# The first down projection of a decoder trunk: three column blocks token-major with seven block products in 17 chunks, results turned through DRAM

## The chip, the cores and the metric

The kernel runs on one core of one Trainium2 chip. It is one launch. The metric is the device time of that launch in microseconds, as the median of several runs. Before the change it is 2175.9 us (three runs, 2174.73 to 2176.43 us).

## The reference, cut to what matters

The reference computes a decoder trunk of two layers on 256 tokens of 2048 features, all in float32: a gated mixer layer, a convolutional feed-forward network (FFN), a shared key and value side, an attention layer, a second FFN, and a last RMS norm. The change is in the last step of the first FFN:

```
h = xn @ w_up                                    # [256, 11264]
h = conv(h);  gate, val = split(h)               # each [256, 5632]
return (silu(gate) * val) @ w_down               # [256, 5632] @ [5632, 2048], added to the residual
```

What follows it at once is the shared key side and the attention layer, which read the residual through two RMS norms with gains of their own (`kv_norm`, `b_norm`).

## The kernel before, in words

**Number format.** Every float32 operand of a matrix product is split into a rounded part and a remainder (`hi`, `lo`, type fp32r). A product of two operands is three matmuls: rounded by rounded, rounded by remainder, remainder by rounded. A weight matrix comes as chunks of 128 x 1024 floats (512 KB). ScalarE writes the rounded part of a chunk (L110), VectorE the remainder (L111), TensorE then has 24 matmuls of 256 columns for it.

**Two layouts.** In a *feature-major* block (`feat_block`) the weights are the stationary operand and the 256 tokens stream past; 256 output features come out as rows. In a *token-major* block (`tok_block`, `seven_block`) the activations are stationary and 512 weight columns stream past; tokens come out as rows. The residual `h` is kept feature-major, in 16 tiles of 128 features (`kt`), until the second FFN's end.

**What sets the order.** All weight chunks of the program are one list of items (`Stream`). The loop `run` goes through the list: at item *i* it loads item *i*+6, splits item *i*+3 and multiplies item *i*. Then it advances every pending generator by one `yield`: those are the evictions, norms and exchanges that follow a block. Each engine runs what it is given strictly in that order. An item made by `then` has no chunk: it calls a function (at its load or its multiply step), takes a place in the list, and advances no generator. There are four buffers for split chunks and four for loaded ones, three PSUM buffers for block results.

**Wide matmuls.** A call of `between` lets the next chunk run its first eight products, and the chunk after it two, as matmuls of 512 columns where others have 256 (two half-products in one instruction, or two of 256 columns in one).

**The first down projection.** `down0` is eight feature-major blocks of 11 chunks. At the end of block *p*, `residual` adds the result to two tiles of `h` (L394), multiplies them by the next gain and splits them into `X1` (`prep`, L309 on ScalarE, L310 on VectorE), and adds their squares to `acc` (L374, L379). After the last block, `token_scale` sums `acc` over features on TensorE (L407). The query projection `b_q`, token-major, reads `X1` right behind it.

**The second down projection** (`down1`) is done differently already: 1536 of its columns are three token-major blocks by `seven_block`, the rest `short_block` and `last_block`. In a block of 22 chunks, some chunks (`SUMMED`: one in the first block, eight in each of the others) are multiplied as a 2 x 2 block matrix product with seven products in place of eight (the scheme of Strassen and Winograd). Such a chunk is two items: nine matmuls on the chunk's own columns, twelve on sums of its columns; 21 in place of 24. VectorE makes the column sums (`weight_sums`, L492, L494, L495) and both items are split (L88, L89). The sums on the activation side are made once (`all_sums`, L471 to L481) and are kept in the room of `X1`. The results of `down1` stay token-major, since `h` has been turned by then.

**Turning.** `blocks_turned` transposes 32 x 32 blocks on VectorE (L853), `rows_out` writes the result to DRAM by four DMAs from SyncE's queue (L860), `rows_in` reads it back by one (L864). The mixer, the attention and `residual_by_token` use this way.

Of the kernel before, what the change touches and what calls it, by code (L numbers as in the profile page):

```python
# [10 lines left out]
F32 = mybir.dt.float32  # L11
F32R = mybir.dt.float32r
I32 = mybir.dt.int32
AF = mybir.ActivationFunctionType
# [162 lines left out]
def build(ctx, tc, d, out):  # L177
# [44 lines left out]
    def feat_block(src, x, K, done):  # L222

        box = {}
        n = K // 4
        for c in range(n):
            def mult(hi, lo, c=c):
                if c == 0:  # L230
                    box["ps"], box["both"] = main_ps(), False
                ps, xx, wide = box["ps"], x(), wide_next()
                box["both"] |= wide > 0

                def rounded(j, m):
                    nonlocal wide
                    w = hi[:, j * 256 + m * P:j * 256 + (m + 1) * P]
                    kt = 4 * c + j
                    if wide > 0:
                        mm(ps[:, m, :], w, xx[:, kt, :], kt == 0, False)  # L240
                        wide -= 1
                    else:
                        for half in range(2):
                            mm(ps[:, m, :T], w, xx[:, kt, half * T:(half + 1) * T], kt == 0 and half == 0, False)

                def remainder(j, m):
                    kt = 4 * c + j
                    mm(ps[:, m, :T], lo[:, j * 256 + m * P:j * 256 + (m + 1) * P], xx[:, kt, :T],
                       False, kt == K - 1)

                for product in (rounded, remainder):
                    for j in range(4):
                        for m in range(2):
                            product(j, m)
                if c == n - 1:
                    s.start(done(box["ps"], box["both"]))
            s.chunk(src[c], mult, FEAT_AT)
# [48 lines left out]
    def prep(dst, kt, gain):  # L306

        g = column(gain + kt)
        nc.scalar.activation(dst[:, kt, :T], h[:, kt, :], AF.Copy, scale=g)  # L309
        nc.vector.scalar_tensor_tensor(dst[:, kt, T:], h[:, kt, :], g, dst[:, kt, :T].bitcast(F32),  # L310
                                       op0=OP.mult, op1=OP.subtract)
# [78 lines left out]
    def residual(p, gain, scale=token_scale):  # L390

        def done(ps, both):
            hh = h[:, 2 * p:2 * p + 2, :]
            nc.vector.tensor_tensor(hh, hh, ps[:, :, :T], op=OP.add)  # L394
            if both:
                nc.vector.tensor_tensor(hh, hh, ps[:, :, T:], op=OP.add)
            for kt in (2 * p, 2 * p + 1):
                prep(X1, kt, gain)
            square_into_acc(p)
            yield  # L400
            if p == 7:
                yield from scale()
        return done
# [79 lines left out]
    def all_sums():  # L483
        for _ in range(4):
            yield
        for q in range(0, len(SUMMED), 2):
            yield from sums_of_blocks(q, SUMMED[q])
# [78 lines left out]
    def sums_into_residual(blk):  # L566
# [14 lines left out]
            state["summed"] += 1  # L581
        return done

    def short_block(src, x, K, done):

        n, box = K // 4, {}
        for c in range(n):
            def mult(hi, lo, c=c):
                if c == 0:
                    box["ps"] = main_ps()[:, :, :T]  # L590
                for tb in range(2):
                    short_products(box["ps"][:, tb, :], c, tb, x, K, hi, lo)
                if c == n - 1:
                    s.start(done(box["ps"]))
            s.chunk(src[c], mult, TOK_AT)
        return box
# [251 lines left out]
    def blocks_turned(src):  # L848


        n = src.shape[1]
        turned = ph.temp("turned", [P, 512])[:, :n * P].rearrange("p (c h j) -> p c h j", c=4, h=n)
        nc.vector.transpose(turned.rearrange("p c h j -> p h c j"), src.rearrange("p h (c i) -> p h c i", c=4))  # L853
        return turned.rearrange("p c h j -> p c (h j)")

    def rows_out(key, turned):

        way = dram.tile([4, 32, 4, turned.shape[2]], F32, name=f"way_{key}", tag=f"way_{key}")
        for r in range(4):
            nc.sync.dma_start(way[:, :, r, :].rearrange("c i x -> i c x"), turned[32 * r:32 * r + 32])  # L860
        return way

    def rows_in(dst, way):
        nc.sync.dma_start(dst, way.rearrange("c i r x -> (c i) r x"))  # L864
# [231 lines left out]
        return done  # L1096


    state = {"normed": False, "layer": 0, "v": 0, "done": 0, "gates": 0, "mixed": 0, "scaled": 0, "summed": 0, "wide": [8, 2]}
    cd = dram.tile([NH, T], F32, name="cd")  # L1100

    nc.scalar.dma_start(col[:, :C_KVNORM], d["col"][:, :C_KVNORM])
# [18 lines left out]
    for p in range(8):  # L1121
        feat_block(d["a_out"][4 * p:4 * p + 4], mlp_x2, KD, residual(p, C_FNORM, row_scale))
    ffn_up(0)
    for p in range(8):
        feat_block(d["down0"][11 * p:11 * p + 11], ffn_h, KF, residual(p, C_BNORM))

    s.then(at_mult=lambda: s.start(kv_operand()))
    for blk in range(4):
# [33 lines left out]
def tok_chunks(w):  # L1162

    K, N = w.shape
    a = w.reshape(K // 256, 2, P, N // 512, 512)
    return np.ascontiguousarray(a.transpose(3, 0, 2, 1, 4)).reshape(-1, P, CHUNK)
# [50 lines left out]
```

## Time and profile before

| | |
|---|---|
| median of 3 runs | 2175.9 us |
| the profiled execution's own time | 2175.67 us |
| its span, first to last instruction | 2173.8 us |
| TensorE matmul busy | 2164.6 us, 18689 instructions |
| VectorE busy | 1536.1 us (71%) |
| ScalarE busy | 1162.4 us (53%) |
| granted TensorE clock | 0.999 |
| DMA, mean | 206 GB/s |
| first down projection on TensorE | 753.54 to 992.90 us |
| second down projection on TensorE | 1932.24 to about 2166 us |

The busy time of an engine is read from the page's first part. A matmul's duration in the trace (276 ns for 256 columns) contains its way through the array; matmuls overlap, so their pace is read from the distance of their starts in the timeline. A line number such as L111 stands for the helper that records the operation, so one line can cover work of many stages.

### The profile page before, as it was taken

The page shows a single profiled execution, that of the slowest core. Times are in us where ns is not written, and L with a number is a line of the kernel's source. Part 1 is how long each engine was busy: PE and PEld are TensorE (multiplying, and loading weights), DVE is VectorE, ACT ScalarE, POOL GpSimd, SP SyncE. Part 2 cuts the span into 40 slices and gives each one's busy share as a digit, 9 for nine tenths or more (in the row PEclk, how much of TensorE's full clock was granted, in tenths as well). Part 3 has the DMA queues.
Part 4 walks back from the last instruction along what each step waited for, and adds up shares of the span by engine and source line. Part 5 has one row for each costly group of instructions (what it writes and reads, how often), then busy time and mean ns, then how long its engine had stood idle before and what let it go on. Part 6 is the DMA issues. An engine that isn't in the chain of part 4 may idle for free.

```text
span 2173.8 us, 45113 instructions
## 1 busy us (share of the span) xinstructions
PE 2164.6 (100%) x18689; PEld 2149.0 (99%) x18689; DVE 1536.1 (71%) x2188; ACT 1162.4 (53%) x1560; POOL 26.4 (1%) x46
## 2 busy tenths in 40 slices
PE   9999999999999999999999999999999999999998
PEld 9999999999999999999999999999999999999998
DVE  6696687777777745556787676678777777778884
ACT  6665555555555544444545665446555555555553
POOL 0000000000000000000001200000000000000000
PEclk9999999999999999999999999999999999999999
DMA  9686566666666666666777776667766666665674
GB/s 313 190 237 205 192 201 195 186 202 186 201 190 197 194 198 194 193 195 180 252 233 260 238 222 196 192 215 221 243 194 194 194 194 194 195 191 179 204 219 149
DMA packets 153230, 447.32 MB, mean 206 GB/s; under 512 B 25584, under 2 KB 44800, under 8 KB 152640
## 3 DMA queue, kind: packets, MB, share of 16 engines
q1 hardware_dynamic: 151488, 440.48, 64.6%
q0 software_dynamic: 1072, 3.41, 0.6%
q8 instruction: 146, 2.39, 0.5%
q10 hardware_dynamic: 464, 0.55, 0.1%
q14 instruction: 60, 0.49, 0.1%
HBM read 430.72 MB, written 13.65 MB: 204 GB/s over the span
## 4 chain that ended last, share of the span: by engine, by line
PE 100%; DVE 0%; ACT 0%; POOL 0%; issue 0%; DVEq 0%; POOLq 0%
PE ps L212 98%; PE mp L1074 0%; PE mp L682 0%; PE ps L1068 0%; PE ps L1069 0%; PE ps L1067 0%; PE mp L1073 0%; DVE h L649 0%; PE mp L407 0%; ACT sq L436 0%; PE mp L212 0%; DVE h L435 0%; DVE h L644 0%; ACT fin_t L636 0%; POOL ident L1109 0%
## 5 line engine op out<-in xcount | busy, mean ns | idle before, releaser
L111 DVE TENSOR_TENSOR wlo<-raw,whi 128x1024 fp32r<-128x1024 f32 x761 | 925.0, 1221 | 387.9 <-ACT whi L110 383.4
L110 ACT ACTIVATE whi<-raw 128x1024 fp32r<-128x1024 f32 x761 | 800.7, 1058 | 680.0 <-PE ps L212 592.8
L212 PE MATMUL ps<-X,whi 128*128 128x256 f32 (+1 forms) x6476 | 824.0, 279 | 0.0
L212 PEld LDWEIGHTS ps<-X,whi 128*128 128x128 f32 x6476 | 776.2, 188 | 6.5
L212 PE MATMUL ps<-X,wlo 128*128 128x256 f32 x3328 | 445.2, 276 | 0.0
L212 PEld LDWEIGHTS ps<-X,wlo 128*128 128x128 f32 x3328 | 409.8, 188 | 1.6
L212 PE MATMUL ps<-whi,ffn_H 128*128 128x256 f32 (+1 forms) x1232 | 200.9, 277 | 0.0
L212 PE MATMUL ps<-whi,X 128*128 128x256 f32 (+1 forms) x1136 | 183.3, 279 | 0.0
L212 PE MATMUL ps<-ffn_H,whi 128*128 128x256 f32 x1408 | 173.9, 276 | 0.0
L212 PEld LDWEIGHTS ps<-whi,ffn_H 128*128 128x128 f32 x1232 | 172.8, 188 | 0.4
L824 DVE SCALAR_TENSOR_TENSOR ffn_room<-ffn_room,col 128x255 f32<-128x255 f32 x352 | 161.8, 480 | 6.4
L212 PEld LDWEIGHTS ps<-ffn_H,whi 128*128 128x128 f32 x1408 | 166.1, 188 | 0.0
L212 PE MATMUL ps<-whi,att_X 128*128 128x256 f32 (+2 forms) x970 | 164.4, 285 | 0.0
L212 PEld LDWEIGHTS ps<-whi,X 128*128 128x128 f32 x1136 | 155.3, 188 | 1.4
L212 PE MATMUL ps<-wlo,ffn_H 128*128 128x256 f32 (+1 forms) x615 | 138.9, 277 | 0.0
L212 PEld LDWEIGHTS ps<-whi,att_X 128*128 128x128 f32 x970 | 135.3, 188 | 3.5
L388 DVE TENSOR_TENSOR ffn_room<-ps,rB 128x512 f32<-128x512 f32 x76 | 52.5, 691 | 116.2 <-PE ps L212 116.2
L820 ACT ACTIVATE ffn_room<-ffn_room,col 128x256 f32<-128x256 f32 x176 | 96.3, 595 | 50.0 <-DVE ffn_room L388 50.0
L212 PE MATMUL ps<-wlo,X 128*128 128x256 f32 (+1 forms) x566 | 116.7, 279 | 0.0
L212 PE MATMUL ps<-wlo,att_X 128*128 128x256 f32 (+2 forms) x476 | 105.5, 286 | 0.0
L212 PEld LDWEIGHTS ps<-wlo,ffn_H 128*128 128x128 f32 x615 | 101.1, 188 | 0.1
L212 PE MATMUL ps<-ffn_H,wlo 128*128 128x256 f32 x704 | 94.1, 276 | 0.0
(199 smaller groups left out, 1517.2 us busy)
## 6 DMA issues: line engine op xcount, KB each, us to landing
raw<-up SPq DMA_DIRECT2D x352, 512.0 KB, 4.1
raw<-down SPq DMA_DIRECT2D x154, 512.0 KB, 4.2
raw<-a_in_u SPq DMA_DIRECT2D x32, 512.0 KB, 4.3
raw<-a_out SPq DMA_DIRECT2D x32, 512.0 KB, 4.0
raw<-b_q SPq DMA_DIRECT2D x32, 512.0 KB, 4.8
raw<-kvf_v SPq DMA_DIRECT2D x32, 512.0 KB, 4.8
raw<-b_g SPq DMA_DIRECT2D x32, 512.0 KB, 4.6
raw<-b_out SPq DMA_DIRECT2D x32, 512.0 KB, 3.8
```

The lines of the kernel that those rows point to most:

```text
L110: self.nc.scalar.activation(h, raw, AF.Copy)
L111: self.nc.vector.tensor_tensor(l, raw, h.bitcast(F32), op=OP.subtract)
L212: nc.tensor.matmul(o, a, b, start=start, stop=stop, skip_group_check=True)
L388: nc.vector.tensor_tensor(a, src, rB[:, None, :].to_broadcast([P, 2, T]), op=OP.mult)
L820: nc.scalar.activation(c[:, m, :], a[:, m, :], AF.Identity, scale=w[2], bias=column(C_CONVB + l * 2 * KF + f))
L824: nc.vector.scalar_tensor_tensor(c[:, m, n:], a[:, m, :T - n], w[k], c[:, m, n:], op0=OP.mult, op1=OP.add)
```

## The change

The columns of `w_down[0]` are divided. The first 1536 are laid out token-major and are done by three calls of `seven_block`, as in the second down projection, with the same choice of chunks: 1 + 8 + 8 = 17 of 66 chunks are done with seven block products. The last 512 columns stay two feature-major blocks (*p* = 6 and 7) with `residual` as before.

The results of the three blocks come out token-major and the residual is feature-major, so they are turned: `sums_apart` first combines the block sums into a tile `Y` and adds the plain products (L593 to L604 of the changed kernel), `blocks_turned` and `rows_out` send each half of 128 tokens to DRAM, and `rows_added` reads it back and adds it to `h` (L621). That is six round trips. `residual_prepared` does for the twelve tiles of `h` what `residual` does at a block's end (`prep`, squares into `acc`), one step at a time, during the two feature-major blocks.

Five `then` items are new: `between` and the start of `all_sums` ahead of the three blocks, `between` and the start of `residual_prepared` behind them, and `check_prepared`, which asserts while the program is built that all twelve tiles are prepared, behind the last block.

```diff
@@ -580,6 +580,64 @@
             nc.vector.tensor_tensor(hh[:, :, T:], hh[:, :, T:], one[:, 0::2, :], op=OP.add)
             state["summed"] += 1
         return done
+
+    def sums_apart(blk):
+
+
+        box = {}
+
+        def sums(m):
+            Y = ph.temp("apart", [P, 4, T], bufs=1)
+            nc.scalar.activation(Y[:, 1, :], m[:, 0, :T], AF.Copy)
+            yield
+            nc.vector.tensor_tensor(Y[:, 0, :], Y[:, 1, :], m[:, 0, T:], op=OP.add)
+            nc.vector.tensor_tensor(Y[:, 3, :], Y[:, 0, :], m[:, 1, T:], op=OP.subtract)
+            yield
+            nc.vector.tensor_tensor(Y[:, 0::2, :], m[:, 1:, :T].to_broadcast([P, 2, T]), Y[:, 0::3, :], op=OP.subtract)
+            box["Y"] = Y
+
+        def done(ps):
+            while "Y" not in box:
+                yield
+            for tb in range(2):
+                z = box["Y"][:, 2 * tb:2 * tb + 2, :].rearrange("p a b -> p (a b)")
+                nc.vector.tensor_tensor(z, z, ps[:, tb, :], op=OP.add)
+                yield
+                turned = blocks_turned(z.rearrange("p (h x) -> p h x", h=4))
+                yield
+                s.start(rows_added(blk, tb, rows_out(f"d{blk}{tb}", turned)))
+                yield
+
+        return done, sums
+
+    def rows_added(blk, tb, way):
+        for _ in range(3):
+            yield
+        rows = ph.temp("drows", [P, 512]).rearrange("p (r x) -> p r x", r=4)
+        rows_in(rows, way)
+        for _ in range(5):
+            yield
+        hh = h[:, 4 * blk:4 * blk + 4, tb * P:(tb + 1) * P].rearrange("p h (r j) -> p r h j", r=4)
+        nc.vector.tensor_tensor(hh, hh, rows.rearrange("p r (h j) -> p r h j", h=4), op=OP.add)
+        state["added"] += 1
+
+    def residual_prepared():
+
+        for p in range(6):
+            while state["added"] < 2 * (p // 2 + 1):
+                yield
+            for kt in (2 * p, 2 * p + 1):
+                prep(X1, kt, C_BNORM)
+                yield
+            sq = small.tile([P, 2, T], F32, name="sq", tag="sq", bufs=2)
+            nc.scalar.activation(sq, h[:, 2 * p:2 * p + 2, :], AF.Square)
+            yield
+            if p == 0:
+                nc.vector.tensor_tensor(acc, sq[:, 0, :], sq[:, 1, :], op=OP.add)
+            else:
+                for i in range(2):
+                    nc.vector.tensor_tensor(acc, acc, sq[:, i, :], op=OP.add)
+        state["prepared"] = True
 
     def short_block(src, x, K, done):
 
@@ -1096,7 +1154,11 @@
         return done
 
 
-    state = {"normed": False, "layer": 0, "v": 0, "done": 0, "gates": 0, "mixed": 0, "scaled": 0, "summed": 0, "wide": [8, 2]}
+    def check_prepared():
+        assert state["prepared"]
+
+    state = {"normed": False, "layer": 0, "v": 0, "done": 0, "gates": 0, "mixed": 0, "scaled": 0, "summed": 0, "added": 0,
+             "prepared": False, "wide": [8, 2]}
     cd = dram.tile([NH, T], F32, name="cd")
 
     nc.scalar.dma_start(col[:, :C_KVNORM], d["col"][:, :C_KVNORM])
@@ -1121,8 +1183,15 @@
     for p in range(8):
         feat_block(d["a_out"][4 * p:4 * p + 4], mlp_x2, KD, residual(p, C_FNORM, row_scale))
     ffn_up(0)
-    for p in range(8):
-        feat_block(d["down0"][11 * p:11 * p + 11], ffn_h, KF, residual(p, C_BNORM))
+    s.then(at_mult=between)
+    s.then(at_mult=lambda: s.start(all_sums()))
+    for blk in range(3):
+        seven_block(blk, d["down0"][22 * blk:22 * blk + 22], order_of(blk), *sums_apart(blk))
+    s.then(at_mult=between)
+    s.then(at_mult=lambda: s.start(residual_prepared()))
+    for p in (6, 7):
+        feat_block(d["down0s"][11 * p - 66:11 * p - 55], ffn_h, KF, residual(p, C_BNORM))
+    s.then(at_mult=lambda: check_prepared())
 
     s.then(at_mult=lambda: s.start(kv_operand()))
     for blk in range(4):
@@ -1198,7 +1267,8 @@
     }
 
     order = np.arange(D).reshape(4, 4, 4, 32).transpose(0, 2, 1, 3).reshape(-1)
-    arrays["down0"] = feat_chunks(np.asarray(f_w_down)[0])
+    down0 = np.asarray(f_w_down)[0]
+    arrays["down0"], arrays["down0s"] = tok_chunks(down0[:, :1536]), feat_chunks(down0[:, 1536:])
     down1 = np.asarray(f_w_down)[1][:, order]
     arrays["down1"], arrays["down1s"] = tok_chunks(down1[:, :1536]), feat_chunks(down1[:, 1536:])
     arrays["final"] = np.asarray(final_norm).reshape(1, D)[:, order]
```

**VectorE around the end of the down projection.** The rows are those of VectorE at the last chunks of `down0` and the first of `b_q`. `raw_11849`, `raw_11879` and `raw_11909` are the first three chunks of `b_q` before the change, `raw_12044`, `raw_12076` and `raw_12104` after it; L394 is the addition of the last block to `h`, which waits for the block's last matmul. Before:

```order
L111 TENSOR_TENSOR wlo_11882<-raw_11791,whi_11881 128x1024
L111 TENSOR_TENSOR wlo_11938<-raw_11849,whi_11937 128x1024
L111 TENSOR_TENSOR wlo_11968<-raw_11879,whi_11967 128x1024
L394 TENSOR_TENSOR h_73<-h_73,ps_11676 128x512
L310 SCALAR_TENSOR_TENSOR X1_74<-h_73,col_71,X1_74 128x256 x2
L379 TENSOR_TENSOR acc_75<-acc_75,sq_12000 128x256 x2
L111 TENSOR_TENSOR wlo_12007<-raw_11909,whi_12006 128x1024
L111 TENSOR_TENSOR wlo_12013<-raw_11935,whi_12012 128x1024
```

With the change:

```order
L639 TENSOR_TENSOR acc_75<-acc_75,sq_12102 128x256 x2
L111 TENSOR_TENSOR wlo_12135<-raw_12044,whi_12134 128x1024
L394 TENSOR_TENSOR h_73<-h_73,ps_11828 128x512
L310 SCALAR_TENSOR_TENSOR X1_74<-h_73,col_71,X1_74 128x256 x2
L379 TENSOR_TENSOR acc_75<-acc_75,sq_12167 128x256 x2
L111 TENSOR_TENSOR wlo_12174<-raw_12076,whi_12173 128x1024
L111 TENSOR_TENSOR wlo_12180<-raw_12104,whi_12179 128x1024
```

The second chunk of `b_q` stood ahead of L394 and now stands behind it and the four operations that follow it, because the item of `check_prepared` takes one of the three places by which the split runs ahead. ScalarE's rows moved in the same way: `whi_12173`, the rounded part of the second chunk, stands behind both L309 and the square L374.

**VectorE and SyncE's queue at the end of the first block.** Before, VectorE at the end of the first feature-major block:

```order
L111 TENSOR_TENSOR wlo_9595<-raw_9502,whi_9594 128x1024
L394 TENSOR_TENSOR h_73<-h_73,ps_9287 128x512
L310 SCALAR_TENSOR_TENSOR X1_74<-h_73,col_71,X1_74 128x256 x2
L376 TENSOR_TENSOR acc_75<-sq_9627 128x256
L111 TENSOR_TENSOR wlo_9633<-raw_9532,whi_9632 128x1024
L111 TENSOR_TENSOR wlo_9664<-raw_9562,whi_9663 128x1024
```

With the change, at the end of the first token-major block (`apart` is `Y`, `room` holds the column sums, the first L604 waits for the block's last matmul):

```order
L596 TENSOR_TENSOR ffn0_apart_9918<-ps_9892,ffn0_apart_9918 128x2x256
L604 TENSOR_TENSOR ffn0_apart_9918<-ffn0_apart_9918,ps_9287 128x512
L89 TENSOR_TENSOR wlo_9989<-ffn0_room_9954,whi_9988 128x1024
L911 STREAM_TRANSPOSE ffn0_turned_10017<-ffn0_apart_9918 128x4x4x32
L111 TENSOR_TENSOR wlo_10022<-raw_9920,whi_10021 128x1024
L492 TENSOR_TENSOR ffn0_room_10056<-raw_9952 128x512
L494 TENSOR_TENSOR ffn0_room_10056<-raw_9952,ffn0_room_10056 128x256
L495 TENSOR_TENSOR ffn0_room_10056<-raw_9952,ffn0_room_10056 128x256
L89 TENSOR_TENSOR wlo_10061<-raw_9952,whi_10060 128x768
L604 TENSOR_TENSOR ffn0_apart_9918<-ffn0_apart_9918,ps_9287 128x512
L89 TENSOR_TENSOR wlo_10078<-ffn0_room_10056,whi_10077 128x1024
L911 STREAM_TRANSPOSE ffn0_turned_10093<-ffn0_apart_9918 128x4x4x32
```

SyncE's queue held nothing but loads of `down0` there; with the change it has, at the same place:

```order
L78 DMA raw_10019<-down0 128x1024
L918 DMA way_d00_10049<-ffn0_turned_10017 32x4x128 x4
L78 DMA raw_10054<-down0 128x1024
L78 DMA raw_10075<-down0 128x1024
L918 DMA way_d01_10123<-ffn0_turned_10093 32x4x128 x4
L78 DMA raw_10128<-down0 128x1024
L922 DMA ffn0_drows_10143<-way_d00_10049 128x512
L78 DMA raw_10145<-down0 128x1024
L78 DMA raw_10195<-down0 128x1024
L922 DMA ffn0_drows_10225<-way_d01_10123 128x512
```

The adds and transposes of the result stand between the splits of the next block's chunks, and the writes and reads of the round trip stand between its loads: `raw_10128` is behind the second write, `raw_10227`, the load that follows these rows, behind the second read.

## The prediction

> **What bounds the kernel now.** I read the page's busy times first, then who TensorE waited for, then the pace of its matmuls in the stages concerned.
>
> ```profile
> PE 2164.6 (100%) x18689; PEld 2149.0 (99%) x18689; DVE 1536.1 (71%) x2188; ACT 1162.4 (53%) x1560; POOL 26.4 (1%) x46
> PE mp L682 <- POOL ident L1109: 1.5, 1, 1.5
> ```
>
> TensorE (PE) works all through; the second row is its only wait, 1.5 us at the start. So time goes only where TensorE gets less work, a better pace or a new wait. The pace, from the starts in its timeline at the end of the first down projection:
>
> ```profile
> 987.46 1.98 PE L212 MATMUL ps<-ffn_H,whi 128*128 128x256 f32 x16
> 990.18 1.98 PE L212 MATMUL ps<-ffn_H,whi 128*128 128x256 f32 x16
> 992.90 0.40 PE L212 MATMUL ps<-whi,X 128*128 128x256 f32 x2
> 998.56 0.50 PE L407 MATMUL mp<-ones,acc 128*128 128x1 f32 x4
> ```
>
> A chunk of 24 matmuls takes 990.18 - 987.46 = 2.72 us, 113.3 ns each. The first two chunks of `b_q` (48 matmuls) take 998.56 - 992.90 = 5.66 us, 117.9 ns each: a slower pace. The timeline shows it elsewhere too, where the weights change from streaming to stationary, and it lasts until the next wide matmuls:
>
> ```profile
> 93.57 2.04 PE L212 MATMUL ps<-X,whi 128*128 128x256 f32 x16
> 96.39 2.05 PE L212 MATMUL ps<-X,whi 128*128 128x256 f32 x16
> ```
>
> Here a chunk takes 2.82 us.
>
> **The matmuls removed.** 17 chunks have 21 matmuls in place of 24, so 51 fewer. The second down projection runs the same three blocks already; its rows tell whether such matmuls keep the pace and whether anything stalls:
>
> ```profile
> 1932.24 0.39 PE L212 MATMUL ps<-whi,ffn_H 128*128 128x512 f32 x1
> 1934.09 0.63 PE L212 MATMUL ps<-whi,ffn_H 128*128 128x256 f32 x4
> 2105.85 0.50 PE L212 MATMUL ps<-whi,ffn_H 128*128 128x256 f32 x3
> ```
>
> In the last row the first two matmuls end the third block (its last product, two of 256 columns) and the third starts the next block, 0.23 us later, at 2106.08. The three blocks are 66 x 24 - 51 = 1533 matmuls of 256 columns and took 173.84 us; at 113.3 ns they are 173.74 us. So they run at full pace with no stall in them, and 51 x 113.3 ns = **5.78 us** goes. The surplus of **0.10 us** is the wide start: its first eight products take 1934.09 - 1932.24 = 1.85 us, 0.231 each, against 0.227 for two matmuls of 256. I charge it to the first new `between`.
>
> The second new `between` stands ahead of a feature-major block. The nearest rows are the first chunks of the first up projection, wide as well:
>
> ```profile
> 282.61 2.02 PE L212 MATMUL ps<-X,whi 128*128 128x512 f32 x8
> 285.41 2.00 PE L212 MATMUL ps<-X,whi 128*128 128x512 f32 x14
> 288.16 1.98 PE L212 MATMUL ps<-X,whi 128*128 128x256 f32 x16
> ```
>
> Two chunks took 5.55 us where the full pace gives 5.44: **0.11 us**. Without it this block would keep the slow pace, 0.10 us for each of its chunks.
>
> The Trainium skill's page "TensorE: Matmul & The Clock Gate", section "Back-to-back issue gap", gives about 131 ns for a matmul of 512 columns in a sustained stream of weight loads and matmuls. By that, the ten wide products of each `between` would gain about 10 x (227 - 131) ns, together 1.9 us, and the time would be 2169.7 us. The trace says 231 ns, so I give that case 1 in 100.
>
> **VectorE and ScalarE in the three blocks.** Rows of the second block of the second down projection, by form (idle time behind the second bar), then the busy times of that stretch by engine (PE, PEld, DVE, ACT), then the transposes of the attention:
>
> ```profile
> L111 DVE TENSOR_TENSOR wlo<-raw,whi 128x1024 fp32r<-128x1024 f32 x14 | 16.9, 1222 | 3.9 <-ACT whi L110 3.9
> L89 DVE TENSOR_TENSOR wlo<-ffn_room,whi 128x1024 fp32r<-128x1024 f32 x8 | 9.8, 1226 | 2.9 <-ACT whi L88 2.9
> L89 DVE TENSOR_TENSOR wlo<-raw,whi 128x768 fp32r<-128x768 f32 x9 | 8.6, 950 | 0.0
> L492 DVE TENSOR_TENSOR ffn_room<-raw 128x512 f32<-128x512 f32 x8 | 5.5, 685 | 0.0
> L495 DVE TENSOR_TENSOR ffn_room<-raw,ffn_room 128x256 f32<-128x256 f32 x8 | 3.4, 425 | 0.3
> L448 DVE TENSOR_TENSOR h<-h,ps 128x512 f32<-128x512 f32 x2 | 1.4, 684 | 0.0
> 1991.80:2048.90 57.10, 57.10 (x506) 57.10 (x506) 49.73 (x64) 30.73 (x35) 0.00 (x0) 1.00 0.66 203
> L853 DVE STREAM_TRANSPOSE att_turned<-att_big x32: 578/645/715, 1025.2 to 1292.9; 128x512 f32<-128x512 f32 x16, 128x384 f32<-128x384 f32 x16
> ```
>
> A seven-product chunk costs VectorE 1.23 + 0.95 + 0.69 + 2 x 0.43 = 3.73 us against 21 x 0.1133 = 2.38 us on TensorE; a plain one 1.22 against 2.72. Over the block, DVE is busy 49.73 of 57.1 us. In the first layer the splits and sums are the same. What handles a block's result differs: two combinations of 256 columns (0.43 each), one of 512, two additions of products and two of rows (0.69 each), two transposes (0.65) = 5.6 us. The second layer's, with seven operations of 0.69 and two of 0.43, cost 5.7 us. So VectorE is no busier than where it already kept up, and I charge nothing; TensorE's work is the cover, and without it a block would pay up to those 5.6 us. The sums on the activations stand behind an up projection in both layers, and the rows from 1932.24 on show that they cost nothing there. At a block's end, though, only three items are split ahead of the addition that waits for the block's last matmul, so the tightest item behind it has to be looked at.
>
> It is the one whose load (`raw_10128`) stands behind the second DRAM write. From the block's end, VectorE does two operations of 0.69, then 1.23, 0.65, 1.22, the three sums 1.54, 0.95, 0.69, 1.23 and 0.65: 9.5 us, about 10 with a wait for a free buffer. Then:
>
> ```profile
> 1493.12 1.78 SPq L860 DMA_DIRECT2D way_h<-ffn_turned  x4
> raw<-down SPq DMA_DIRECT2D x154, 512.0 KB, 4.2
> DMA to landing us min/median/max: 1.8/4.4/7.0
> ```
>
> Four writes issue in 1.8 us, the load goes out by 12.3, lands 4.2 us later at 16.5, and its remainder is ready at 18.9 (ScalarE 1.1, VectorE 1.2). TensorE gets there after five plain and three seven-product chunks, 5 x 2.72 + 3 x 2.38 = 20.7 us, and needs the remainder 0.2 us later. About 2 us are spare: nothing charged, for the reads too, which have five items to land. The last row is the spread of the second layer's `way_h` transfers; its 7.0 us in place of 4.2 for the load would need 0.7 us more than there is. That is a rival below.
>
> **The preparation** of twelve tiles moves into the two feature-major blocks. VectorE has 2.72 - 1.22 us spare in each of 22 chunks; ScalarE, with 1.1, more. Nothing waits for the tiles before `b_q`. Nothing charged; without that cover twelve L310 and eleven additions to `acc` of 0.45 us each (rows below) would be 10 us of VectorE.
>
> **The start of `b_q`: a new wait.** Before the change its first two chunks were split before L394. The rows of VectorE, then ScalarE there:
>
> ```profile
> 987.85 1.23 DVE L111 TENSOR_TENSOR wlo<-raw,whi 128x1024 fp32r<-128x1024 f32 x1 [1.50 <-ACT whi L110]
> 993.11 0.69 DVE L394 TENSOR_TENSOR h<-h,ps 128x512 f32<-128x512 f32 x1 [4.03 <-PE ps L212]
> 994.37 0.89 DVE L310 SCALAR_TENSOR_TENSOR X<-h,col,X 128x256 fp32r<-128x256 f32 x2 [0.58 <-ACT X L309]
> 995.29 0.89 DVE L379 TENSOR_TENSOR acc<-acc,sq 128x256 f32<-128x256 f32 x2
> 996.25 2.36 DVE L111 TENSOR_TENSOR wlo<-raw,whi 128x1024 fp32r<-128x1024 f32 x2
> 993.83 0.91 ACT L309 ACTIVATE X<-h,col 128x256 fp32r<-128x256 f32 x2 [6.01 <-DVE h L394]
> 994.64 0.62 ACT L374 ACTIVATE sq<-h 128x512 f32<-128x512 f32 x1
> 995.17 2.94 ACT L110 ACTIVATE whi<-raw 128x1024 fp32r<-128x1024 f32 x3
> ```
>
> The split that follows was the third chunk's and had time. With `check_prepared` in the list it is the second's. Taking TensorE's end of the last block (992.90) as zero: the chain L394, L309, square, rounded part ends at 996.25 - 992.90 = 3.35; the remainder follows and ends at 3.35 + 1.22 = 4.57. TensorE does the first chunk at 117.9 ns in 2.83 us; it waits 0.52 for the rounded part, does two matmuls (0.24), and in a token-major block the remainder is needed right then, at 3.59: it waits 0.98. Together 1.50, and about 0.05 to hand over, **1.55 us**. Queued behind are the third chunk's parts, ready 1.2 us later while TensorE has 22 matmuls more to do: no second wait. Bounds: 1.3 if the additions finish earlier than in these rows, 1.9 if the hand-over costs as much as from TensorE to L394, 0.2 each way. At the other two borders the same thinning of the lead is covered: behind the up projection the second layer's rows above show no loss, and ahead of the last feature-major blocks VectorE has 2 x 0.69 + 1.22 = 2.6 us to do and the remainder is needed only after 24 + 16 matmuls, 4.5 us.
>
> **Sum.** -5.78 + 0.10 + 0.11 + 1.55 = -4.0 us. The profiled execution's own 2175.67 us becomes 2171.65; from the median of the runs, 2175.9, **2171.9 us**, 0.18% less. What this kernel's measurement can tell from no change is 0.2%, 4.35 us: the forecast lies just inside it.
>
> **Rivals.**
>
> *No wait at `b_q`* (chance 0.11). If the second chunk's parts come before TensorE needs them, 5.6 us are saved: 2170.3 us. For it: no wait of this kind exists in the trace, so its price is inferred. Against: both engines work strictly in order, and L394 cannot start before the block's last matmul.
>
> *A late load behind the DRAM write, and slow pace* (0.09); slower than before. Place: the eighth chunk after the first and the second block's end. It decides once that load lands more than about 6.2 us after its issue. At 7.0 us, 0.7 us twice is 1.4. If a wait puts TensorE into the slow pace, it stays there until the next wide matmuls: 504 - 183 = 321 matmuls of one block and 504 of the next, 825 x 4.6 ns = 3.8 us. Together 5.2: 2177.1 us. For it: no `between` stands in the blocks. Against: 2 us are spare, and no row shows slow pace after a wait.
>
> *A second wait of the size of the first* (0.08), ahead of the last feature-major blocks or once more at `b_q`: 1.55 more, 2173.4 us. Against: the 1.9 us of cover just named.
>
> *The page's wide matmuls* (0.01), 2169.7, and anything else (0.02). The forecast has 0.69.
>
> **Range and chances.** The bounds of the wait (1.3 to 1.9) put the forecast between 2171.6 and 2172.2 us; half the spread of the three runs, 0.85 us, on either side makes it 2170.8 to 2173.1. To leave out no more than 2 in 10, it reaches to the first and third rival: 2169.8 to 2174.4. Faster by over 0.2% (below 2171.55): nearly all of the first rival and a quarter of the forecast, 0.30. Slower by over 0.2%: 0.05. Within: 0.65.
>
> **What would show it.** Right: in the changed profile the three blocks from TensorE's first `whi,ffn_H` to its first `ffn_H,whi` after take 173.8 us with no wait; TensorE waits about 0.5 us for ScalarE's L110 and 1.0 for VectorE's L111 in the second chunk of `b_q`, and the distance from its first `b_q` matmul to L407 grows from 5.66 to about 7.2 us. Wrong: a chunk pace above 2.72 us in the blocks, a wait of SyncE's reads that TensorE feels, or no wait at `b_q`.

## The result, and the profile after

The changed kernel takes **2172.1 us** in the median (22 runs, 2171.00 to 2175.85 us), beside 2175.8 us for the kernel before, run alongside (22 runs, 2174.71 to 2178.47 us). The ratio is 0.9983, with a 95% interval of 0.9976 to 0.9989: 3.7 us less, and 0.17% by the ratio. The interval leaves out 1, though the difference is just inside the 0.2% that the prediction took as the least that can be told from no change. The profiled execution took 2171.64 us with a span of 2169.9 us; before it was 2175.67 and 2173.8 us.

The busy times of the page (each engine's busy us, share of the span, instructions) and TensorE's waits (total, times, longest) of the changed kernel:

```profile
PE 2159.5 (100%) x18618; PEld 2142.6 (99%) x18618; DVE 1597.3 (74%) x2298; ACT 1180.9 (54%) x1584; POOL 26.4 (1%) x46
PE ps L212 <- DVE wlo L111: 0.8, 1, 0.8
PE ps L212 <- ACT whi L110: 0.4, 1, 0.4
```

TensorE is still busy all through. Beside the 1.5 us at the start it has two waits that it did not have before, one for a remainder and one for a rounded part, and VectorE has 61 us more work, none of which shows beyond these two. Their place is the start of `b_q`. The changed kernel's timeline of TensorE at the stage borders (start, duration, idle time ahead in brackets):

```profile
753.53 0.39 PE L212 MATMUL ps<-whi,ffn_H 128*128 128x512 f32 x1
927.38 2.02 PE L212 MATMUL ps<-ffn_H,whi 128*128 128x512 f32 x8
930.17 2.00 PE L212 MATMUL ps<-ffn_H,whi 128*128 128x512 f32 x14
932.92 1.98 PE L212 MATMUL ps<-ffn_H,whi 128*128 128x256 f32 x16
987.32 0.40 PE L212 MATMUL ps<-whi,X 128*128 128x256 f32 x2
990.68 0.50 PE L212 MATMUL ps<-whi,X 128*128 128x256 f32 x2 [0.37 <-ACT whi L110]
991.94 0.50 PE L212 MATMUL ps<-wlo,X 128*128 128x256 f32 x2 [0.76 <-DVE wlo L111]
992.27 0.62 PE L212 MATMUL ps<-whi,X 128*128 128x256 f32 x4
992.95 0.62 PE L212 MATMUL ps<-whi,X 128*128 128x256 f32 x4
994.54 0.50 PE L407 MATMUL mp<-ones,acc 128*128 128x1 f32 x4
```

The three token-major blocks take 927.38 - 753.53 = 173.85 us, the two feature-major blocks 987.32 - 927.38 = 59.94 us, and from the first matmul of `b_q` to L407 it is 7.22 us. From the stage's first matmul to L407 the changed kernel needs 241.01 us; the kernel before needed 998.56 - 753.54 = 245.02. The whole difference of 4.0 us between the two profiled executions lies in this stretch. The brackets hold 0.37 and 0.76 us, but the distance of the starts is what counts: a matmul of 256 columns is listed with some 0.28 us, though the next one starts 0.113 us after it.

The same border on VectorE (first two rows) and ScalarE of the changed kernel:

```profile
987.52 0.69 DVE L394 TENSOR_TENSOR h<-h,ps 128x512 f32<-128x512 f32 x1 [6.75 <-PE ps L212]
990.66 3.50 DVE L111 TENSOR_TENSOR wlo<-raw,whi 128x1024 fp32r<-128x1024 f32 x3
989.58 3.89 ACT L110 ACTIVATE whi<-raw 128x1024 fp32r<-128x1024 f32 x4
```

VectorE stood idle for 6.75 us ahead of L394, because its order puts L394 in front of the split of the second `b_q` chunk and L394 has to wait for the last matmul of the block. On ScalarE the first of the four rounded parts of the L110 row, begun at 989.58 and 1.06 us long, is ready at 990.64, and TensorE starts at 990.68. On VectorE the first of the three remainders, begun at 990.66, is ready 1.22 us later at 991.88, and TensorE goes on at 991.94. This is not lack of capacity: both engines had time, but their order did not let them use it.

### The profile page after: what moved, and what is told of

It is laid out like the page before. It is cut to its first block, busy times and chain, and to the rows that moved or that the text cites. A ratio compares the mean times of both kernels' runs of the same rounds, so it can differ in the third digit from the quotient of the medians.

```text
span 2169.9 us, 45154 instructions
## 1 busy us (share of the span) xinstructions
PE 2159.5 (100%) x18618; PEld 2142.6 (99%) x18618; DVE 1597.3 (74%) x2298; ACT 1180.9 (54%) x1584; POOL 26.4 (1%) x46
## 4 chain that ended last, share of the span: by engine, by line
PE 99%; DVE 0%; ACT 0%; POOL 0%; issue 0%; DVEq 0%; POOLq 0%
PE ps L212 98%; PE mp L1132 0%; PE mp L740 0%; PE ps L1126 0%; PE ps L1127 0%; PE ps L1125 0%; PE mp L1131 0%; DVE wlo L111 0%; ACT whi L110 0%; DVE h L707 0%; PE mp L407 0%; ACT sq L374 0%; ACT sq L436 0%; PE mp L212 0%; DVE h L435 0%
## 5 line engine op out<-in xcount | busy, mean ns | idle before, releaser
L111 DVE TENSOR_TENSOR wlo<-raw,whi 128x1024 fp32r<-128x1024 f32 (+1 forms) x744 | 902.9, 1219 | 322.6 <-ACT whi L110 318.5
L110 ACT ACTIVATE whi<-raw 128x1024 fp32r<-128x1024 f32 (+1 forms) x744 | 782.8, 1058 | 631.0 <-PE ps L212 523.6
L212 PE MATMUL ps<-whi,ffn_H 128*128 128x256 f32 (+1 forms) x2112 | 342.0, 277 | 0.0
L212 PEld LDWEIGHTS ps<-whi,ffn_H 128*128 128x128 f32 x2112 | 292.5, 188 | 0.7
L212 PE MATMUL ps<-wlo,ffn_H 128*128 128x256 f32 (+1 forms) x1054 | 229.3, 277 | 0.0
L212 PE MATMUL ps<-whi,X 128*128 128x256 f32 (+1 forms) x1272 | 209.4, 279 | 0.4 <-ACT whi L110 0.4
L212 PEld LDWEIGHTS ps<-wlo,ffn_H 128*128 128x128 f32 x1054 | 169.2, 188 | 0.2
L212 PEld LDWEIGHTS ps<-wlo,X 128*128 128x128 f32 x634 | 100.3, 188 | 1.3 <-DVE wlo L111 1.0
L212 PEld LDWEIGHTS ps<-wlo,att_X 128*128 128x128 f32 x476 | 75.4, 188 | 1.0
L88 ACT ACTIVATE whi<-ffn_room 128x1024 fp32r<-128x1024 f32 x34 | 36.2, 1064 | 54.1 <-DVE ffn_room L495 43.1
```

Of the source, the lines that this page charges most:

```text
L88: self.nc.scalar.activation(hi[:, :n], src, AF.Copy)
L110: self.nc.scalar.activation(h, raw, AF.Copy)
L111: self.nc.vector.tensor_tensor(l, raw, h.bitcast(F32), op=OP.subtract)
L212: nc.tensor.matmul(o, a, b, start=start, stop=stop, skip_group_check=True)
```

## The experiments

The kernel before ran beside each group on the same chip: 2175.96 us beside "One item less", "One item more", "No wide products" and "Plain products", 2176.06 us beside the others. Beside the changed kernel it took 2175.8 us, so a comparison of a median below with the changed kernel's 2172.1 us is good to some 0.3 us; the ratios and the distances within a profile are firmer.

**One item less.** The assertion is merged into the item behind it, so the list of items is one shorter at the border to `b_q`.

```diff
-    s.then(at_mult=lambda: check_prepared())
-    s.then(at_mult=lambda: s.start(kv_operand()))
+    s.then(at_mult=lambda: (check_prepared(), s.start(kv_operand())))
```

> The assert moves into the item that starts the key operand, so one item fewer stands between the last down-projection block and the query projection; nothing else changes. Theory (the wait at the query projection comes from the item, which takes one of the three places of the lead): the second chunk is split before the last addition again, TensorE's two waits (0.5 and 1.0 us) are gone, the way from the first query matmul to the sum of squares is 5.66 us as before the change, and the time is 1.55 us below the changed kernel's 2172.1: 2170.5 us, 0.9975 of before. Rival (the preparation of twelve tiles, moved to just ahead, keeps VectorE and ScalarE late): the waits stay at more than half their size, 2171.5 to 2172.1 us.

Measured: 2170.57 us, ratio 0.9978 (0.9969 to 0.9986). TensorE's only wait, and the border in its timeline:

```profile
PE mp L740 <- POOL ident L1171: 1.5, 1, 1.5
988.48 0.40 PE L212 MATMUL ps<-whi,X 128*128 128x256 f32 x2
994.14 0.50 PE L407 MATMUL mp<-ones,acc 128*128 128x1 f32 x4
```

Both waits are gone and the distance is 5.66 us again, 1.56 less than in the changed kernel; the median is 1.54 lower. So the wait needs the item.

**The item alone, without the change.** The kernel before, with one empty item at that place.

```diff
+    s.then(at_mult=lambda: None)
     s.then(at_mult=lambda: s.start(kv_operand()))
```

> The kernel before, with one empty item put ahead of the one that starts the operand of the keys and values; nothing of the change is in it. Theory (the wait at b_q comes from the number of items between the last block and the split, not from token-major columns or their preparation): the same two waits of TensorE as in the changed kernel, 0.4 to 0.5 us on ScalarE L110 and 0.8 to 1.0 us on VectorE L111, the stretch from the first b_q matmul to the first of L407 goes from 5.66 to 7.22 us, and the time from 2175.9 to 2177.4 us, a ratio of 1.0007. Rival (the wait comes from what the change prepares or leaves on VectorE and ScalarE at that place): no wait, 5.66 us, 2175.9 us.

Measured: 2177.6 us, ratio 1.0007 (0.9998 to 1.0016), beside 2176.06. Beside the one at the start TensorE has the same two waits, 0.4 us for a rounded part and 0.8 us for a remainder. Its timeline:

```profile
992.80 0.40 PE L212 MATMUL ps<-whi,X 128*128 128x256 f32 x2
1000.03 0.50 PE L407 MATMUL mp<-ones,acc 128*128 128x1 f32 x4
```

From 992.80 to 1000.03 it is 7.23 us, where the changed kernel has 7.22. The medians alone would not settle it, since the interval holds 1; the two waits and the stage's own distance do. Nothing of the token-major blocks or the preparation is needed for the wait.

**One item more.** The changed kernel with another empty item.

```diff
     s.then(at_mult=lambda: check_prepared())
+    s.then(at_mult=lambda: None)
```

> One more empty item at the same place: the double dose. Theory: the first query chunk is split behind the last addition too. Its rounded part is ready 3.35 us after the last block's end and its remainder at 4.6, where TensorE needs them at 0 and 0.2: it waits about 3.4 and 1.0 us, 4.4 in all, 2.85 more than in the changed kernel: 2175.0 us. Rival (load of the preparation, not the place in the list): no more than 0.3 us is added, 2172.1 to 2172.4 us.

Measured: 2176.61 us, ratio 1.0004 (0.9995 to 1.0013): 1.6 us above the expected 2175.0. TensorE's timeline, and then the windows of that stretch (length, busy us of PE, PEld, DVE, ACT and POOL, then the granted clock, the share of the DMA engines and GB/s):

```profile
989.93 0.51 PE L212 MATMUL ps<-whi,X 128*128 128x256 f32 x2 [3.19 <-ACT whi L110]
991.19 0.80 PE L212 MATMUL ps<-wlo,X 128*128 128x256 f32 x2 [0.76 <-DVE wlo L111]
991.79 1.05 PE L212 MATMUL ps<-whi,X 128*128 128x256 f32 x4
993.07 1.05 PE L212 MATMUL ps<-whi,X 128*128 128x256 f32 x4
998.09 0.50 PE L407 MATMUL mp<-ones,acc 128*128 128x1 f32 x4
991.19:994.30 3.11, 3.11 (x14) 3.11 (x15) 3.11 (x3) 1.53 (x2) 0.00 (x0) 0.50 0.62 192
```

The chain of waits came as forecast: with the last block's end (986.58, by the pace of its last matmuls) as zero, TensorE goes on with the rounded part at 3.35 and with the remainder at 4.61. What the theory did not have is the last row: behind the waits the granted clock was 0.50 for about 3.1 us. From 991.79 to 993.07 six matmuls took 1.28 us, 213 ns each in place of 113. That is the missing 1.4 us of this stage. The Trainium skill's page "TensorE: Matmul & The Clock Gate", section "Why this matters for your kernels", warns of idle gaps of TensorE above about 3 us because the clock then drops to half. The trace agrees here, with 3.35 us from the last block's end to the first matmul of `b_q` (3.19 in the bracket), and so does the changed kernel, whose waits of 0.53 and 1.03 us left the clock at 1.00.

**No wide products.** The two new calls of `between` are made empty.

```diff
-    s.then(at_mult=between)
+    s.then(at_mult=lambda: None)
     s.then(at_mult=lambda: s.start(all_sums()))
...
-    s.then(at_mult=between)
+    s.then(at_mult=lambda: None)
     s.then(at_mult=lambda: s.start(residual_prepared()))
```

> The two new items that start wide matmuls are kept as empty items, so the lead stays as it is and only the wide matmuls are gone. Theory (after the weights change sides the pace stays slow until the next wide matmuls): the three blocks run at 117.5 to 117.9 ns a matmul, 180.1 to 180.7 us in place of 173.85, and the two feature-major blocks at 2.82 us a chunk, 62.0 in place of 59.9; together about 8.6 us more than the changed kernel: 2180.7 us, slower than before the change. Rival (the slow pace ends by itself after a few chunks): 0.5 us more at most, 2172.6 us.

Measured: 2180.98 us, ratio 1.0024 (1.0015 to 1.0034). TensorE's timeline of this kernel at the start of the three blocks, at their end, and at `b_q`:

```profile
753.00 0.40 PE L212 MATMUL ps<-whi,ffn_H 128*128 128x256 f32 x2
933.56 2.05 PE L212 MATMUL ps<-ffn_H,whi 128*128 128x256 f32 x16
995.75 0.40 PE L212 MATMUL ps<-whi,X 128*128 128x256 f32 x2
998.26 0.39 PE L212 MATMUL ps<-whi,X 128*128 128x256 f32 x2
```

The blocks take 180.56 us, 117.8 ns for each of 1533 matmuls, and the feature-major ones behind them 995.75 - 933.56 = 62.19 us, 2.25 more than with the wide start. So the two calls, which cost 0.1 us each, are worth 8.9 us by the medians: without them the change would be slower than the kernel before. The slow pace lasted for 243 us, so it does not end by itself after a few chunks. But it needs no wide matmul to end: the last two rows are 22 matmuls of `b_q` apart and 2.51 us, where the slow pace would give 2.59. From the fifth matmul on (996.22) the distance is 113.3 ns again, with no wide matmul and no wait ahead of it, only the change from feature-major to token-major.

**Plain products.** All 66 chunks are done with eight products; the blocks stay token-major and their results are turned in the same way.

```diff
+    def plain_apart(blk):
+        def done(ps):
+            Y = ph.temp("apart", [P, 4, T], bufs=1)
+            for tb in range(2):
+                z = Y[:, 2 * tb:2 * tb + 2, :].rearrange("p a b -> p (a b)")
+                nc.scalar.activation(z, ps[:, tb, :], AF.Copy)
+                yield
+                turned = blocks_turned(z.rearrange("p (h x) -> p h x", h=4))
+                yield
+                s.start(rows_added(blk, tb, rows_out(f"d{blk}{tb}", turned)))
+                yield
+        return done
...
-    s.then(at_mult=lambda: s.start(all_sums()))
+    s.then(at_mult=lambda: None)
     for blk in range(3):
-        seven_block(blk, d["down0"][22 * blk:22 * blk + 22], order_of(blk), *sums_apart(blk))
+        tok_block(d["down0"][22 * blk:22 * blk + 22], ffn_h, plain_apart(blk), KF)
```

> The three blocks stay token-major and their results are turned by way of DRAM, but all 66 chunks are done with eight products: no sums of activations, of weights or of products. Theory (the gain is the 51 matmuls, all else costs what was charged): 5.78 us more than the changed kernel, the blocks take 179.6 us, the wait at the query projection stays at 1.5: 2177.9 us, 1.0010 of before. Rival (the gain comes from the layout, or the seven products cost TensorE something that hides part of their gain): 2172.1 us in the first case, 2179 or more in the second.

Measured: 2177.95 us, ratio 1.0010 (1.0001 to 1.0019). TensorE's blocks run from

```profile
753.11 0.39 PE L212 MATMUL ps<-whi,ffn_H 128*128 128x512 f32 x1
932.74 2.02 PE L212 MATMUL ps<-ffn_H,whi 128*128 128x512 f32 x8
```

179.63 us, 5.78 more than with the seven products: 51 matmuls of 113.3 ns. The median is 5.84 us above the changed kernel's. The turned layout alone, without the seven products, is 2.0 us slower than the kernel before by the medians; the wait and the two wide starts are 1.8 us of that.

**No round trip.** The tile that VectorE turned is added to `h` as it stands: this kernel leaves out the exchange of 32 x 32 blocks between partitions, with its writes and reads.

```diff
-                s.start(rows_added(blk, tb, rows_out(f"d{blk}{tb}", turned)))
+                s.start(rows_added(blk, tb, turned))
...
-        rows = ph.temp("drows", [P, 512]).rearrange("p (r x) -> p r x", r=4)
-        rows_in(rows, way)
+        rows = way
```

> The changed kernel without the way by DRAM: the tile that VectorE turned is added to h as it stands, so the exchange of 32-blocks between partitions is left out, and with it its writes and reads. Theory (the trip is hidden wholly behind TensorE's products): the time of the changed kernel, 2172.1 us within 0.3, a ratio of 0.9983; waits of TensorE only at b_q, 0.4 and 0.8 us. Rival (the trip delays a weight load or a result that TensorE waits for): 0.5 us or more less, 2171.6 us or below.

Measured: 2171.62 us, ratio 0.9979 (0.9970 to 0.9989). This median is at the rival's limit, 0.5 us below the changed kernel's, and the intervals overlap widely. The stages decide; TensorE's timeline in this kernel:

```profile
752.75 0.39 PE L212 MATMUL ps<-whi,ffn_H 128*128 128x512 f32 x1
926.60 0.62 PE L212 MATMUL ps<-ffn_H,whi 128*128 128x512 f32 x2
```

173.85 us for the blocks, 59.94 us for the feature-major ones behind them, 7.24 us from `b_q` to L407: to 0.02 us the distances of the changed kernel. The round trips are hidden.

The profiled execution is the longest of the ten, 2173.65 us, 2.0 us above the median. The time is lost further on, in the middle of `b_q`:

```profile
1013.15 0.62 PE L212 MATMUL ps<-whi,X 128*128 128x256 f32 x4
1013.60 0.45 PE L212 MATMUL ps<-wlo,X 128*128 128x256 f32 x2
1013.89 0.63 PE L212 MATMUL ps<-whi,X 128*128 128x256 f32 x4
```

Four matmuls take 0.45 us, 113 ns each; then one distance is 0.17 us, a delay of 0.06; and the next four take 0.47 us, to 1014.36. From there the pace is 118 ns up to 1086 us, a stretch that the changed kernel runs at 113.3; 2.9 us are lost, of which the earlier start of this profile (752.75 in place of 753.53) hides 0.8. No change of sides lies there: the slow pace began behind a short delay. Longer delays at the same place, 0.24 and then 0.11 us in the profile of the last experiment below, were followed by the full pace.

**The writes tripled.** Each turned tile is written three times, two of them to tiles that nobody reads, so that the weight load behind the second write is late.

```diff
                 turned = blocks_turned(z.rearrange("p (h x) -> p h x", h=4))
                 yield
+                for copy in "xy":
+                    rows_out(f"{copy}{blk}{tb}", turned)
                 s.start(rows_added(blk, tb, rows_out(f"d{blk}{tb}", turned)))
```

> The changed kernel with each turned tile written to DRAM three times, two of them to tiles that nobody reads; what is computed stays. It makes the queue of SyncE late by two writes for each half. Theory (the weight load behind the second write has about 2 us to spare, and a wait of TensorE ends the slow pace): the load goes out some 17.8 us after a block's end, not 12.3, and TensorE waits about 3.4 us after blocks 1 and 2, in all about 7 us: 2179 us. Rival (after a wait the pace is slow until the next wide matmuls): 3.8 us more, 2183 us. Other rival (the load has far more to spare than 2 us, or the writes don't hold the queue): no wait behind the blocks, 2172.1 us.

Measured: 2181.82 us, ratio 1.0029 (1.0019 to 1.0039). First what the load does in the changed kernel: its issue on SyncE's queue, its rounded part, its remainder, and the matmuls that need them.

```profile
825.08 0.39 SPq L78 DMA_DIRECT2D raw<-down  x1
830.45 1.06 ACT L110 ACTIVATE whi<-raw 128x1024 fp32r<-128x1024 f32 x1 [1.50 <-DMA raw<-down]
831.54 1.22 DVE L111 TENSOR_TENSOR wlo<-raw,whi 128x1024 fp32r<-128x1024 f32 x1 [1.34 <-ACT whi L110]
834.10 0.39 PE L212 MATMUL ps<-wlo,ffn_H 128*128 128x256 f32 x2
```

The remainder is ready at 831.54 + 1.22 = 832.76 and wanted at 834.10: 1.3 us to spare. With the writes tripled the blocks begin at 752.77, 0.76 us earlier, and the load goes out at 829.81: 5.5 us later than in the changed kernel, and TensorE waits. Its rows after the first and then the second block, and last the clock behind the second wait (windows, as above):

```profile
833.36 0.28 PE L212 MATMUL ps<-whi,ffn_H 128*128 128x256 f32 x1
834.70 0.51 PE L212 MATMUL ps<-whi,ffn_H 128*128 128x256 f32 x2 [1.06 <-ACT whi L110]
835.96 0.51 PE L212 MATMUL ps<-wlo,ffn_H 128*128 128x256 f32 x2 [0.76 <-DVE wlo L111]
836.30 0.62 PE L212 MATMUL ps<-whi,ffn_H 128*128 128x256 f32 x4
893.89 0.28 PE L212 MATMUL ps<-whi,ffn_H 128*128 128x256 f32 x1
896.41 0.50 PE L212 MATMUL ps<-whi,ffn_H 128*128 128x256 f32 x2 [2.25 <-ACT whi L110]
897.67 0.50 PE L212 MATMUL ps<-wlo,ffn_H 128*128 128x256 f32 x2 [0.76 <-DVE wlo L111]
898.01 0.63 PE L212 MATMUL ps<-whi,ffn_H 128*128 128x256 f32 x4
902.08 0.44 PE L212 MATMUL ps<-whi,ffn_H 128*128 128x256 f32 x2
898.20:900.70 2.50, 2.50 (x16) 2.50 (x16) 2.10 (x5) 1.45 (x2) 0.00 (x0) 0.61 0.97 388
```

From 833.36 to 836.30 TensorE started five matmuls, 0.57 us at full pace: 2.37 us lost. From 893.89 to 898.01, five again: 3.55 lost. The theory had 3.4 for each. Behind the first wait six matmuls take 0.68 us (to 836.98), the full pace, and the clock stays at 1.00. Behind the second the 22 matmuls from 898.01 to 902.08 take 4.07 us in place of 2.49, at a granted clock of 0.61 in the window: 1.58 more. The blocks last 182.81 us in all, 8.96 more than in the changed kernel; these three terms are 7.5 of it. Of the other 1.5, about 1.2 are four delays of 0.15 to 0.43 us near the two waits that the view of waits does not list.

So the queue does hold the load back, as the theory said, and the pace behind these waits is full once the clock is back, against the first rival; the time lies near that rival's 2183 for another reason, the second half-clock stretch in this study. No single gap reaches 3 us there: the longest is 2.41. The profiled execution is the shortest of the eight (2180.45 to 2184.79 us); what the longer ones lost is not shown.

**Two more wide starts, and the merged item.** `feat_block` gets a switch (its definition is left out below) that calls `between` at the first chunk of the first layer's `a_in_u`, and `b_q` gets a call ahead of it.

```diff
-    s.then(at_mult=lambda: check_prepared())
-    s.then(at_mult=lambda: s.start(kv_operand()))
+    s.then(at_mult=lambda: (check_prepared(), between(), s.start(kv_operand())))
...
-        feat_block(d["a_in_u"][4 * p:4 * p + 4], lambda: X1, KD, u_done(p))
+        feat_block(d["a_in_u"][4 * p:4 * p + 4], lambda: X1, KD, u_done(p), p == 0)
```

> The changed kernel with the empty item merged into the one behind it, and two more wide products of the kind that line 212's 512-column matmul makes: one at the first chunk of the second up projection, one just ahead of b_q. Theory (wide matmuls end the slow pace wherever it runs, and cost about 0.11 us each): no wait at b_q; the first five chunks of the up projection go from 2.82 to 2.72 us, 0.5 us less for the 0.11 us of the product; at b_q, which takes 5.66 us at the slow pace, 24 chunk-parts at 113.3 instead of 117.7 ns give 0.2 us for the 0.11 us. Sum against the item merged alone: 0.4 to 0.5 us less; time 2170.0 us, a ratio of 0.9973. Rival (the slow pace there ends by itself and the products are paid in full): 2170.8 us, 0.9977.

(The expectation calls `a_in_u` the second up projection; it is the second projection of the first mixer.) Measured: 2169.99 us, ratio 0.9973 (0.9962 to 0.9983), the lowest median of the study. TensorE's timeline in this kernel, at the start of `a_in_u`, five chunks and the mixer's twelve matmuls on, at the start of `b_q`, and at its token sums:

```profile
93.72 2.02 PE L212 MATMUL ps<-X,whi 128*128 128x512 f32 x8
108.84 2.04 PE L212 MATMUL ps<-X,whi 128*128 128x512 f32 x8
987.05 0.39 PE L212 MATMUL ps<-whi,X 128*128 128x512 f32 x1
992.59 0.50 PE L409 MATMUL mp<-ones,acc 128*128 128x1 f32 x4
```

In the changed kernel the same two places of `a_in_u` are

```profile
93.55 2.04 PE L212 MATMUL ps<-X,whi 128*128 128x256 f32 x16
109.12 2.03 PE L212 MATMUL ps<-X,whi 128*128 128x512 f32 x8
```

so that stretch goes from 15.57 to 15.12 us, 0.45 less, and `b_q` to L407 (here L409) from 5.66 with the item merged to 5.54, 0.12 less. Their sum is 0.57 us; this median lies 0.58 below that of the merged item alone. The medians of these two come from different chips and their intervals overlap; the stages carry the reading.

## Why the prediction was right

The forecast was 2171.9 us; the median is 2172.1. From the first matmul of the stage to L407 the sum said 4.02 us less, and the profile shows 4.01. Step by step:

- **The matmuls removed**, 5.78 us: right. With the products put back the blocks take 5.78 us more.
- **The wide starts**, 0.10 and 0.11 us: right. The first three blocks take 173.85 us (173.84 in the second layer), and the first two feature-major chunks 5.54 us, from 927.38 to 932.92. That they are needed was argued from the slow pace elsewhere and is now shown: 8.9 us without them. The reading behind it was too narrow, though. The prediction let the slow pace begin where the weights change sides and last until the next wide matmuls; it also ended without them at `b_q` in "No wide products", and began without a change of sides in the profile of "No round trip".
- **VectorE and ScalarE charged nothing in the blocks**: right. No wait of TensorE lies in them, though VectorE is busy for 146.83 of the 173.85 us. Windows of the blocks, and of the feature-major blocks behind them:

```profile
753.53:927.38 173.85, 173.85 (x1526) 173.41 (x1525) 146.83 (x182) 88.98 (x94) 0.00 (x0) 1.00 0.68 212
927.38:987.32 59.94, 59.94 (x521) 59.50 (x519) 41.99 (x57) 30.34 (x41) 0.00 (x0) 1.00 0.67 212
```

- **The preparation charged nothing**: right. The second row above is its cover: VectorE is busy for 41.99 of 59.94 us, and TensorE does not wait.
- **The load behind the second DRAM write, 2 us to spare**: right in kind, too wide in size behind the first block. There the margin was 1.3 us. The load needed 830.45 - 825.08 = 5.4 us to its rounded part's start where the sum took the 4.2 us of the median transfer. A landing 5.4 + 1.3 = 6.7 us after the issue, where the rival had 6.2, would be felt. Behind the second block the same load took 882.20 to 886.35, 4.2 us, its remainder was ready at 888.67 and wanted at 891.22: 2.5 us. Tripling the writes used up both margins by making the issue later.
- **The wait at `b_q`**, 0.52 + 0.98 + 0.05 = 1.55 us: right, and for the reason given. By starts it is 0.53 and 1.03 us, and the distance to L407 grew by 1.56. Removing the item removes it; the item alone makes it.
- **A term that was not in the sum**: behind the wait TensorE's pace was full. Six matmuls took 992.95 - 992.27 = 0.68 us, where in the kernel before they took 0.70 to 0.71 at this place. The 22 matmuls after the wait thus gained 0.10 us, and restarting cost as much: from 991.94 to 992.27 two matmuls took 0.33 us in place of 0.23. The two cancel, so the sum came out right with a step missing.
- **The rivals.** No wait at `b_q`: its time, 2170.3, is what the merged item gives (2170.57), so its price was right and its condition was not met. The late load: its mechanism exists, its threshold was not crossed, and its second half, that a wait puts TensorE into the slow pace, did not hold for the waits in "The writes tripled", nor for the wait at `b_q` in "No wide products", which was at full pace on both sides of it; but it is not wrong in general, since the slow pace began right behind the delay of 0.06 us in the profile of "No round trip". A second wait did not appear. The 131 ns for 512 columns that the Trainium skill's page "TensorE: Matmul & The Clock Gate", section "Back-to-back issue gap", gives did not appear either. The chunk behind the second new `between`, eight wide products and eight of 256 columns, took 930.17 - 927.38 = 2.79 us, where 8 x 231 + 8 x 113.3 ns are 2.75 us and 131 in place of 231 would make it 1.95.

## What to carry to other kernels

Where a list of items sets how far one engine works ahead, an item that does nothing still costs one place of the lead. Look for the point at which an in-order engine meets an operation that waits for the end of a block, count what is queued in front of it before and after, and take the wait from the chain's durations: here that gave 1.55 us in advance against 1.56 measured. In a kernel bound by one engine, compare the distance of starts from border to border; a difference of 0.02 us between stages can be read where the medians of whole runs differ by 0.5 us. Such a distance is that of one execution, and the pace can differ from one to the next, as the 2 us in "No round trip" show.

## What the hardware showed that was not expected

- A wait can end the slow pace just as wide matmuls do. With 118 ns per matmul ahead of it, two waits of 0.53 and 1.03 us were followed by 113 ns (the changed kernel, and the kernel before with an item added); without the waits ("One item less") 118 ns lasted up to L407. In the kernel with tripled writes, which was at full pace ahead of the wait, it stayed full.
- The slow pace hangs on more than that. It began behind a delay of 0.06 us in one profile, in the middle of a stage (113 ns before, 118 after, 2.9 us lost), and it ended at a change of sides in another (118 ns before, 113 after). What sets it was not tried.
- The granted clock fell to about half behind 3.4 to 4.4 us of idle TensorE with two matmuls in between: 3.35 + 1.03 us in the kernel with one more item, 2.41 + 1.03 us behind the second block of the one with tripled writes. Behind 1.23 + 1.03 us (the latter's first wait) and 0.53 + 1.03 us it stayed at 1.00. Each time it cost 1.4 to 1.6 us more than the wait itself. If the sum of the two gaps decides, the limit lies between 2.3 and 3.4 us; if the longer one does, between 1.2 and 2.4. These runs do not show which.
